# Convolution taps and gate scalings between VectorE, ScalarE and GpSimd, and an earlier second token half, in a hybrid encoder block

## The chip, the cores and the metric

The kernel runs on one core of a Trainium2 chip. The metric is the device time of one execution in microseconds (us); for a kernel with several executions it is their median. The core's engines are TensorE (PE, matrix products and transposes), VectorE (DVE), ScalarE (ACT), GpSimd (POOL) and SyncE (SP, which issues the transfers). Each engine runs its own instructions in program order and waits on semaphores for the others.

## What is computed

One layer of an encoder block, on 1024 tokens of width 1024, all in float32. The part around the change:

```python
h = rms_norm(x, norm1_g)
z = h @ w_in                                   # 1024 x 2560
a, gate, q, k, v = jnp.split(z, splits, axis=-1)   # 512 columns each
u = a * sigmoid(gate)
y = depthwise_conv(u, dw_kernel) + dw_bias     # 31 taps over the tokens, padding 15
conv_out = silu(layer_norm(y, ln_g, ln_b))
q, k = rms_norm per head of 64
attn_out = neighbourhood_attention(q, k, v, rpb)   # 8 heads, 16 rows of 64 tokens
x = x + concat(conv_out, attn_out) @ w_out
h = rms_norm(x, norm2_g)
x = x + (silu(h @ w_gate) * (h @ w_up)) @ w_down
```

## The kernel before

The order of every engine is the order of the code; nothing is rescheduled. All products use split operands: a float32 matrix is held as a high half (a cast) and a low half (the rest), and `mac` (L111 to L114) adds three products: high by high (L112), high by low (L113), low by high (L114). A weight chunk of 128x1024 is loaded raw into one of three buffers; `split` (L104, L108) casts it on ACT and subtracts on POOL, and `take` then issues the load of the chunk three later. The chunks are taken in this order: wk0 to wk3 (the weights of k), then ag10, ag00, ag11, ag01, ag12, ag02, ag13, ag03 (ag1c are gate columns, ag0c value columns of channel chunk c), w00 to w03 (of q), w20 to w23 (of v), then those of w_out. The letters h and l behind a name are its high and low halves, r the raw buffer.

The tokens are worked on in two halves of 512. `h_split` (L258, L259) makes the two halves of the normalised, transposed input for one token half: hT high on ACT, hT low on DVE. The root mean squares of x (tiles of 128 tokens) are not applied to it; they are kept in `r1`, one column for each tile, and applied to the products. `stats1` computes them: for odd tiles with bn_stats on DVE (L264 to L266), for even ones with a Square on ACT (L271), then a Sqrt on ACT (L277) and a reciprocal on DVE (L278). For the gated unit, whose products are channels by tokens, `r_rows` turns four columns of `r1` into a row vector `rb` with four transposes on PE (L287) into a PSUM buffer (tag tp, of two) and a copy on DVE (L288). The same two buffers hold the transposes of q and k (`zt`, L388), which ACT empties (kT at L395, qT at L393).

PE's order in this part: k products of tiles 0 to 3 (first token half); the gated unit of chunk 0, half 0 then half 1, each a gate product (part 0) and a value product (part 1); k tiles 4 to 7; the gated unit of chunks 1 to 3; eight q products (weights w00 to w03); eight v products (w20 to w23); then attention. A product is 24 matmuls into a PSUM bank of 512 columns. Jobs in the list `woven` are taken out between the steps of a product, one after each three matmuls: this is where the transposes of q, k (`head_T`) and the row vector come.

`step(post)` runs behind each product. It does the post-work of the product before, and then calls `side()` once. The post-work of a k or q product (`head_post`) is the squares and a Sqrt on ACT (L366 or L370, L373), three convolution taps on DVE, then zn on DVE (L378 to L381), and it sets the transposes of zn seven places ahead in `woven`. That of a gate product is `gate`: sg = gate x rb on DVE (L440), Sigmoid on ACT (L441), sg x rb on DVE (L442), and taps. That of a value product is `val`: u = value x sg on DVE (L448), and taps.

The convolution of a channel chunk reads u, 128 channels by 1024 tokens. `pump(n)` issues n of DVE's steps: the centre tap into the accumulator cv in PSUM (L312), then one multiply-add for each tap (L317), and at the end u = cv + pa (L322). `side()` issues one tap of the list SIDE: the product on ACT (L342; for the first tap straight into pa, L339) and the addition to pa on POOL (L343). A chunk begins when u of both token halves is there.

Of the kernel before, what the change touches and what calls it, by code (L numbers as in the profile page):

```python
# [8 lines left out]
AF = mybir.ActivationFunctionType  # L9
OP = mybir.AluOpType  # L10
PSUM = bass.MemoryType.PSUM

P = 128
D = 1024
S = 1024
KB = D // P
# [7 lines left out]
NEG = -1e30  # L24
GW = 64
AR = 12
SIDE = (16, 17, 18, 19, 20, 21)
WIN = ((0, 24, 8), (8, 32, 0), (24, 32, 0), (40, 24, 0))


# [37 lines left out]
def build(ctx, tc, a):  # L68
    nc = tc.nc
    pe, act, dve, pool = nc.tensor, nc.scalar, nc.vector, nc.gpsimd  # L70
    sb = ctx.enter_context(tc.tile_pool(name="sb", bufs=1))
# [4 lines left out]
    def T(tag, shape, bufs, name, dt=F32):  # L76
        return sb.tile(shape, dt, tag=tag, bufs=bufs, name=name)

    def G(name, dt=F32):
        return T("G", [P, 1024], 22, name, dt)  # L80
# [7 lines left out]
    def ST(name, dt=F32):  # L88
        return T("st", [P, 512], 5, name, dt)

    def SM(name, n=8):
        return T("sm", [P, 8], 16, name)[:, :n]

    def mm(name):
        return ps.tile([P, 512], F32, tag="mm", bufs=4, name=name)

    def tp(name):
        return ps.tile([P, 512], F32, tag="tp", bufs=2, name=name)

    def cv(name):  # L100
        return ps.tile([P, 1024], F32, tag="cv", bufs=1, name=name)

    def split(hi, lo, src, sub=(pool,)):
        act.copy(hi, src)  # L104
        n = src.shape[-1] // len(sub)
        for i, eng in enumerate(sub):
            sl = slice(i * n, (i + 1) * n)
            eng.tensor_tensor(*[w[..., sl] for w in (lo, src, hi.bitcast(F32))], OP.subtract)  # L108

    def mac(acc, l, r, start, stop):  # L110
        (lh, ll), (rh, rl) = l, r  # L111
        pe.matmul(acc, lh, rh, start=start, stop=False, skip_group_check=True)  # L112
        pe.matmul(acc, lh, rl, start=False, stop=False, skip_group_check=True)  # L113
        pe.matmul(acc, ll, rh, start=False, stop=stop, skip_group_check=True)  # L114


    woven = []

    def weave():
        if woven:  # L120
            woven.pop(0)()
# [12 lines left out]
    def issue():  # L134
        if pos[0] < len(chunks):
            src, name, _, _ = chunks[pos[0]]
            raws[pos[0]] = R(name + "r")
            d = raws[pos[0]]
            if len(src.shape) == 3:
                d = d.rearrange("p (k m) -> p k m", k=src.shape[1])  # L140
            nc.sync.dma_start(d, src)
            pos[0] += 1

    def take(n=1, ahead=True):
        for _ in range(n):
            i = pos[1]
            while pos[0] <= i:
                issue()
            _, _, dst, sub = chunks[i]
            hi, lo = dst()  # L150
            split(hi, lo, raws.pop(i), sub)
            pos[1] += 1
            if ahead and pos[0] < i + 4:
                issue()
# [53 lines left out]
    FIRST, SECOND, ALL = slice(0, 256), slice(256, 512), slice(0, 512)  # L208
# [21 lines left out]
    eps = T("eps", [P, 1], 1, "eps")  # L230
# [22 lines left out]
    r1 = T("r1", [P, 8], 1, "r1")  # L253

    def h_split(h, k, sl):
        src = xr[h, k // 2][:, k % 2, sl]
        hi, lo = [w[:, k, sl] for w in hT[h]]
        act.activation(hi, src, AF.Copy, scale=g1[:, k:k + 1])  # L258
        dve.scalar_tensor_tensor(lo, src, g1[:, k:k + 1], hi.bitcast(F32), OP.mult, OP.subtract)  # L259

    def bn_sum(t):
        st, mv, ss = T("bn", [P, 2, 6], 2, f"sb{t}"), SM(f"sv{t}", 2), SM(f"s1{t}", 1)
        for i in range(2):
            dve.bn_stats(st[:, i], x_t[t][:, i * 512:(i + 1) * 512])  # L264
        dve.bn_aggr(mv, st)
        dve.scalar_tensor_tensor(ss, mv[:, 0:1], mv[:, 0:1], mv[:, 1:2], OP.mult, OP.add)  # L266
        return ss, 1.0
# [6 lines left out]
    def stats1(t):  # L274
        ss, scale = (bn_sum if t % 2 else sq_sum)(t)
        sd = SM(f"sd1{t}", 1)
        act.activation(sd, ss, AF.Sqrt, bias=eps, scale=scale)  # L277
        dve.reciprocal(r1[:, t:t + 1], sd)  # L278
# [3 lines left out]
    def r_rows(h):  # L282
        if not rb:
            rb.append(G("rb"))
        pt = tp(f"rb{h}")
        for i in range(4):
            pe.transpose(pt[:, i * P:(i + 1) * P], r1[:, 4 * h + i:4 * h + i + 1].to_broadcast([P, P]), ident)  # L287
        dve.tensor_copy(rb[0][:, h * 512:(h + 1) * 512], pt)  # L288
# [13 lines left out]
    def span(t):  # L302
        lo, hi = max(0, 15 - t), min(S, S + 15 - t)
        return slice(lo, hi), slice(lo + t - 15, hi + t - 15)

    def conv_taps():
        for c in range(4):
            while len(u) <= c or not u[c][1]:
                yield False
            uc = u[c][0]  # L310
            acc = cv(f"cv{c}")
            dve.tensor_scalar(acc, uc, dwk[:, c, 15:16], dwb[:, c:c + 1], op0=OP.mult, op1=OP.add)  # L312
            yield True
            for t in range(CW):
                if t != 15 and t not in SIDE:
                    o, i = span(t)
                    dve.scalar_tensor_tensor(acc[:, o], uc[:, i], dwk[:, c, t:t + 1], acc[:, o], OP.mult, OP.add)  # L317
                    yield True
            for _ in range(10):
                if len(aside) <= c or not aside[c][1]:  # L320
                    side()
            dve.tensor_tensor(uc, acc, aside[c][0], OP.add)  # L322
            yield True


    aside = []

    def side_taps():
        for c in range(4):
# [4 lines left out]
            aside.append([pa, False])  # L334
            for n, t in enumerate(SIDE):
                o, i = span(t)
# [3 lines left out]
                else:  # L340
                    pr = G(f"pr{c}{t}")
                    act.activation(pr[:, o], uc[:, i], AF.Copy, scale=dwk[:, c, t:t + 1])  # L342
                    pool.tensor_tensor(pa[:, o], pa[:, o], pr[:, o], OP.add)  # L343
                aside[c][1] = n == len(SIDE) - 1
                yield
# [3 lines left out]
    def side():  # L349
        next(sides, None)  # L350

    conv = conv_taps()

    def pump(n):
        for _ in range(n):
            if not next(conv, False):
                return
# [49 lines left out]
    def step(post=None, n_taps=4):  # L407
        todo = pend[:]
        pend.clear()
        if post is not None:  # L410
            pend.append(post)
        behind()
        for f in todo:
            f(n_taps)
        if not todo:
            pump(n_taps)
        side()

    def head_post(n, t, z):
        def f(n_taps):  # L420
            sd = head_sq(n, t, z)
            pump(3)
            zn = head_scale(n, t, z, sd)
            woven.extend([lambda: None] * 6)
            woven.append(lambda: head_T(n, t, zn))
        return f

    def glu_step(c, h, part, accs, extra=None):
        acc = accs[part] = mm(f"gl{c}{h}{part}")
        w = [q.rearrange("p (k m) -> p k m", m=P) for q in wag[1 - part, c][0]]  # L430
        for k in range(KB):
            mac(acc, [q[:, k, :] for q in w], [q[:, k, :] for q in hT[h]], k == 0, k == KB - 1)
            weave()
        if extra:
            extra(0)

        def gate(n_taps):
            sg = accs["sg"] = ST(f"sg{c}{h}")
            row = rb[0][:, h * 512:(h + 1) * 512]
            dve.tensor_tensor(sg, acc, row, OP.mult)  # L440
            act.activation(sg, sg, AF.Sigmoid)  # L441
            dve.tensor_tensor(sg, sg, row, OP.mult)  # L442
            pump(n_taps - 1)

        def val(n_taps):
            if h == 0:
                u.append([G(f"u{c}"), False])
            dve.tensor_tensor(u[c][0][:, h * 512:(h + 1) * 512], acc, accs["sg"], OP.mult)  # L448
            u[c][1] = h == 1
            pump(n_taps)  # L450
        step((gate, val)[part])


# [38 lines left out]
    def behind(n=6):  # L492
        for _ in range(n):
            if aside_dma:
                aside_dma.pop(0)()
# [7 lines left out]
    for kp in range(4):  # L503
# [13 lines left out]
        for j in range(2):  # L517
            for t in range(2):
                k = 2 * kp + j
# [10 lines left out]
    take(1, False)  # L530
    for q in range(4):
        load_xt(1, q, ALL)
    woven.extend([lambda: None] * 4)
    woven.append(lambda: r_rows(0))
    project(1, 3, head_post)
    for t in range(4, 8):
        load_x(t)
    take(1)
    accs = {}
    for part in range(2):  # L540
        glu_step(0, 0, part, accs)
    for k in range(KB):
        h_split(1, k, ALL)
    for t in range(4, 8):
        stats1(t)
    woven.extend([lambda: None] * 4)
    woven.append(lambda: r_rows(1))
    accs = {}
    for part in range(2):
        glu_step(0, 1, part, accs)  # L550
    for t in range(4, 8):
        project(1, t, head_post)
        if t in (4, 6):
# [3 lines left out]
    for c in range(1, 4):  # L557
        for h in range(2):
            accs = {}
# [129 lines left out]
    s1 = score_mm(1)  # L689
# [80 lines left out]
    for i in range(2, 32 + 2):  # L770
# [8 lines left out]
        if i < 32:  # L779
            ss = score_mm(i)  # L780
# [455 lines left out]
```

## Time and profile before

| | us |
|---|---|
| median of three runs | 1087.36 |
| lowest and highest | 1086.7, 1088.07 |
| profiled execution | 1088.63 |
| its span in the trace | 1086.9 |

| engine | busy us | share of the span |
|---|---|---|
| PE | 1058.5 | 97% |
| DVE | 702.1 | 65% |
| ACT | 453.6 | 42% |
| POOL | 382.1 | 35% |

Times in the trace run from the span's start. The stage around the change lies between 30 and 250 us; the gated unit of chunks 1 to 3 between 84.88 and 151.8, the first q product starts at 151.8. Rows of a timeline give the start, the duration, the engine, the line of the kernel, the operation, and in brackets how long the engine was idle before it and what ended that. Rows that say x4 or x7 hold so many instructions.

### The profile page before, as it was taken

To read this page: it belongs to the slowest core of one execution; us is meant where nothing else is said; L and a number is where in the kernel's file an instruction comes from. 1 tells how busy PE (TensorE), PEld (TensorE's weight loads), DVE (VectorE), ACT (ScalarE), POOL (GpSimd) and SP (SyncE) were. 2 spreads that over 40 slices of the span, in tenths; PEclk is the share of its full clock that TensorE was granted. 3 is DMA by queue.
4 is the path that set the end of the run, shared out by engine and by line. 5 is a ranking of instruction groups with operands and counts; after the bars stand their busy time and mean duration, and the time that the engine had idled before them with its cause. 6 is when DMAs were issued, how large, how long until landed. Compare 5 with 4: busy or idle time off the path is not lost.

```text
span 1086.9 us, 14051 instructions
## 1 busy us (share of the span) xinstructions
PE 1058.5 (97%) x5068; PEld 850.6 (78%) x5068; DVE 702.1 (65%) x1054; ACT 453.6 (42%) x993; POOL 382.1 (35%) x299
## 2 busy tenths in 40 slices
PE   7999998999999999999999999999999999999997
PEld 6778886876667788788888888888888888888886
DVE  6577998795675335765645546464564567857883
ACT  6556345825775524542232322323223245433431
POOL 0126374412452201645445444454445300002220
PEclk9999998999999999999999999999999999999999
DMA  9316772144422442123222322322332498624541
GB/s 343 143 45 221 214 197 79 64 160 135 138 86 80 135 136 97 39 74 121 97 95 100 127 97 80 133 97 88 107 110 94 145 326 303 203 80 131 187 151 43
DMA packets 68245, 144.06 MB, mean 133 GB/s; under 512 B 12496, under 2 KB 21200, under 8 KB 67536
## 3 DMA queue, kind: packets, MB, share of 16 engines
q1 hardware_dynamic: 66336, 139.95, 38.5%
q10 hardware_dynamic: 1840, 3.22, 0.9%
q8 instruction: 40, 0.66, 0.3%
q14 instruction: 29, 0.24, 0.1%
HBM read 103.99 MB, written 44.76 MB: 137 GB/s over the span
## 4 chain that ended last, share of the span: by engine, by line
PE 83%; DVE 9%; ACT 4%; issue 2%; DMA 1%; POOL 1%; SPq 0%; ACTq 0%; DVEq 0%; POOLq 0%
PE B L112 6%; PE B L114 6%; PE B L113 6%; DVE cv L317 5%; PE D L112 4%; PE D L114 4%; PE D L113 4%; PE A L112 4%; PE A L114 4%; PE A L113 3%; PE z L112 3%; PE z L113 3%; PE z L114 3%; PE p L637 2%; PE B2d L112 1%
## 5 line engine op out<-in xcount | busy, mean ns | idle before, releaser
L317 DVE SCALAR_TENSOR_TENSOR cv<-u,par,cv 128x1009 f32<-128x1009 f32 (+11 forms) x96 | 122.7, 1278 | 2.7
L104 ACT CAST op<-sr 128x512 fp32r<-128x512 f32 x77 | 47.6, 619 | 51.5 <-PE B2d L114 20.9
L343 POOL TENSOR_TENSOR pa<-pa,pr 128x1022 f32<-128x1022 f32 (+4 forms) x20 | 47.9, 2397 | 59.3 <-ACT pr L342 55.3
L1023 DVE TENSOR_TENSOR g<-B,g 128x512 f32<-128x512 f32 x22 | 15.2, 691 | 80.3 <-PE B L114 80.3
L108 DVE TENSOR_TENSOR op<-sr,op 128x512 fp32r<-128x512 f32 x77 | 56.0, 728 | 16.3 <-ACT op L104 16.3
L1191 POOL TENSOR_TENSOR ou<-ou,resm 128x512 f32<-128x512 f32 x8 | 12.1, 1511 | 143.8 <-DMA resm<-xd 140.6
L1032 ACT ACTIVATE D<-D 128x512 f32<-128x512 f32 x22 | 12.8, 582 | 114.5 <-DVE D L1031 114.5
L1018 DVE TENSOR_TENSOR u<-B,g 128x512 f32<-128x512 f32 x22 | 15.2, 690 | 64.5 <-PE B L114 64.5
L104 ACT CAST op<-wd 128x512 fp32r<-128x512 f32 x66 | 40.9, 619 | 31.7 <-DVE wd L1110 18.5
L108 DVE TENSOR_TENSOR op<-wd,op 128x512 fp32r<-128x512 f32 x66 | 52.5, 796 | 2.2 <-ACT op L104 0.4
L628 POOL TENSOR_SCALAR e<-e,rs 128x288 f32<-128x288 f32 (+1 forms) x64 | 34.3, 548 | 55.3 <-DVE rs L626 25.3
L872 DVE TENSOR_TENSOR ts<-gu,ts 128x512 f32<-128x512 f32 x44 | 53.1, 1208 | 0.8
L1021 ACT ACTIVATE A<-A 128x512 f32<-128x512 f32 x20 | 11.6, 582 | 77.4 <-PE A L114 77.4
L621 ACT ACTIVATE e<-e,mx 128x288 f32<-128x288 f32 (+1 forms) x64 | 36.3, 568 | 8.2 <-DVE mx L619 8.2
L637 PEld LDWEIGHTS p<-ident,e 128*96 128x96 f32 (+1 forms) x192 | 20.0, 133 | 18.6 <-issue 10.3
L872 DVE TENSOR_TENSOR ts<-gu 128x512 f32<-128x512 f32 x22 | 34.1, 1551 | 0.0
L619 DVE CUSTOM_DVE_ANT_0 e<-s,tab 128x288 f32<-128x288 f32 (+1 forms) x64 | 29.8, 503 | 5.9 <-PE s L606 5.4
L637 PE MATMUL p<-ident,e 128*96 128x128 f32 (+1 forms) x192 | 27.5, 279 | 3.9 <-DVE pT L642 2.5
L370 ACT ACTIVATE sq<-z,r 128x64 f32<-128x64 f32 x96 | 28.6, 335 | 2.8 <-PE z L114 2.8
L653 PE MATMUL o<-pT,vw 96*64 96x128 f32 (+1 forms) x384 | 28.0, 281 | 0.0
L606 PE MATMUL s<-kT,qT 64*128 64x288 f32 (+1 forms) x128 | 26.7, 495 | 0.0
L112 PE MATMUL B2d<-op 128*128 128x512 f32 x66 | 25.8, 391 | 0.0
(1033 smaller groups left out, 3470.0 us busy)
## 6 DMA issues: line engine op xcount, KB each, us to landing
gu<-in_gu SPq DMA_DIRECT2D x44, 512.0 KB
sr<-sd SPq DMA_DIRECT2D x77, 256.0 KB
sd<-sd SPq DMA_DIRECT2D x22, 512.0 KB
wd<-in_wd SPq DMA_DIRECT2D x44, 256.0 KB
sd<-g SPq DMA_DIRECT2D x33, 256.0 KB
x<-in_x SPq DMA_DIRECT2D x16, 512.0 KB
xd<-x SPq DMA_DIRECT2D x8, 512.0 KB
resm<-xd SPq DMA_DIRECT2D x16, 256.0 KB
```

The costliest lines, as they stand in the source:

```text
L104: act.copy(hi, src)
L108: eng.tensor_tensor(*[w[..., sl] for w in (lo, src, hi.bitcast(F32))], OP.subtract)
L112: pe.matmul(acc, lh, rh, start=start, stop=False, skip_group_check=True)
L113: pe.matmul(acc, lh, rl, start=False, stop=False, skip_group_check=True)
L114: pe.matmul(acc, ll, rh, start=False, stop=stop, skip_group_check=True)
L317: dve.scalar_tensor_tensor(acc[:, o], uc[:, i], dwk[:, c, t:t + 1], acc[:, o], OP.mult, OP.add)
L343: pool.tensor_tensor(pa[:, o], pa[:, o], pr[:, o], OP.add)
L619: dve.tensor_tensor_reduce(out=e[:, hh], in0=ss[hh], in1=tab[rh, cb][2 * hp + hh], scale=-1.0, scalar=3.0e38, op0=OP.add, op1=OP.min, accu ...
L621: act.activation(e[:, hh], e[:, hh], AF.Exp, bias=mx, scale=-1.0, accum_out=rs[:, hh:hh + 1])
L628: pool.tensor_scalar(es[i][:, hh], es[i][:, hh], rs[:, hh:hh + 1], 1.0, op0=OP.mult, op1=OP.mult)
L637: pe.transpose(pt[:m, g * P:(g + 1) * P], es[i][:, hh, g * m:(g + 1) * m], ident)
L872: dve.tensor_tensor(o, l, r, OP.subtract)
```

## The change

SIDE grows from six taps to nine, so DVE has 21 multiply-adds in each chunk instead of 24. `step` calls `side()` a second time once the side taps of the second chunk have begun. The second scaling in `gate` is on POOL. `gate` and `val` both pump three taps (before: three and four). In the first part, the row vector of half 0 is made straight ahead of the first gate product rather than woven into a k product; the split of the second token half stands around the first gate product, ahead of the post-work that holds the first Sigmoid; the statistics of tiles 4 to 7 are all by bn_stats on DVE, with a single Sqrt and a single reciprocal of four columns; the row vector of half 1 is made right behind the gate product of half 1.

```diff
-SIDE = (16, 17, 18, 19, 20, 21)
+SIDE = (16, 17, 18, 19, 20, 21, 22, 23, 24)
...
-    def bn_sum(t):
-        st, mv, ss = T("bn", [P, 2, 6], 2, f"sb{t}"), SM(f"sv{t}", 2), SM(f"s1{t}", 1)
+    def bn_sum(t, ss=None):
+        st, mv = T("bn", [P, 2, 6], 2, f"sb{t}"), SM(f"sv{t}", 2)
+        ss = SM(f"s1{t}", 1) if ss is None else ss
...
-            for _ in range(10):
+            for _ in range(2 * len(SIDE)):
                 if len(aside) <= c or not aside[c][1]:
                     side()
...
         if not todo:
             pump(n_taps)
         side()
+        if len(aside) > 1:
+            side()
...
             act.activation(sg, sg, AF.Sigmoid)
-            dve.tensor_tensor(sg, sg, row, OP.mult)
-            pump(n_taps - 1)
+            pool.tensor_tensor(sg, sg, row, OP.mult)
+            pump(3)
...
             u[c][1] = h == 1
-            pump(n_taps)
+            pump(3)
...
-    woven.extend([lambda: None] * 4)
-    woven.append(lambda: r_rows(0))
     project(1, 3, head_post)
     for t in range(4, 8):
         load_x(t)
     take(1)
+    r_rows(0)
+    for k in range(4):
+        h_split(1, k, ALL)
     accs = {}
-    for part in range(2):
-        glu_step(0, 0, part, accs)
-    for k in range(KB):
+    glu_step(0, 0, 0, accs)
+    for k in range(4, KB):
         h_split(1, k, ALL)
+    ss = SM("s14", 4)
     for t in range(4, 8):
-        stats1(t)
-    woven.extend([lambda: None] * 4)
-    woven.append(lambda: r_rows(1))
+        bn_sum(t, ss[:, t - 4:t - 3])
+    act.activation(ss, ss, AF.Sqrt, bias=eps)
+    dve.reciprocal(r1[:, 4:], ss)
+    glu_step(0, 0, 1, accs)
     accs = {}
-    for part in range(2):
-        glu_step(0, 1, part, accs)
+    glu_step(0, 1, 0, accs, lambda _: r_rows(1))
+    glu_step(0, 1, 1, accs)
```

## The prediction

> **What bounds the kernel now.** I read the busy shares first, then what TensorE (PE) waits for, then the timeline around those waits, then the busy time by stages.
>
> ```profile
> PE 1058.5 (97%) x5068; PEld 850.6 (78%) x5068; DVE 702.1 (65%) x1054; ACT 453.6 (42%) x993; POOL 382.1 (35%) x299
> ```
>
> PE is busy for 97% of the span, so only two things can move the end: time in which PE waits, and time in which it runs at a lower clock. The waits, by PE line and releaser (us, times, longest):
>
> ```profile
> PE z L112 <- ACT wk0h L104: 6.1, 1, 6.1
> PE zt L388 <- DVE zn L381: 4.8, 1, 4.8
> PE rb L287 <- ACT kT L395: 1.9, 1, 1.9
> PE gl L112 <- ACT hT L258: 0.7, 1, 0.7
> PE gl L113 <- DVE hT L259: 0.3, 1, 0.3
> ```
>
> The first is the start-up, which the change does not touch. The other four, 7.7 us, are what it is about; around the second and third the clock falls too:
>
> ```profile
> 43.71 0.40 PE L114 MATMUL gl<-hT,ag00l 128*128 128x512 f32 x1
> ...
> 55.82 0.40 PE L114 MATMUL gl<-hT,ag00l 128*128 128x512 f32 x1
> 58.16 0.65 PE L287 MATMUL rb<-ident,r 128*128 128x128 f32 x4 [1.94 <-ACT kT L395]
> 58.56 0.48 PE L112 MATMUL gl<-hT,ag00h 128*128 128x512 f32 x1
> 60.72 0.63 PE L112 MATMUL z<-wk0h,hT 128*128 128x512 f32 x1
> 62.42 0.50 PE L113 MATMUL z<-wk0l,hT 128*128 128x512 f32 x1
> 62.76 0.39 PE L114 MATMUL z<-wk0h,hT 128*128 128x512 f32 x1
> 67.19 0.39 PE L112 MATMUL z<-wk0h,hT 128*128 128x512 f32 x1
> ...
> 172.87 1.11 PE L388 MATMUL zt<-ident,zn 128*128 128x128 f32 x4 [4.81 <-DVE zn L381]
> 178.81 0.39 PE L112 MATMUL z<-w01h,hT 128*128 128x512 f32 x1
> 182.75 0.39 PE L112 MATMUL z<-w00h,hT 128*128 128x512 f32 x1
> ```
>
> The columns are start, duration, engine, line, operation, and the wait before it. Matmuls start 0.233 us apart at full clock (the 24 of one product reach from 60.72 to 67.19; the last nineteen steps, from 62.76 on, take 4.43) and 0.425 apart after a wait (four steps from 60.72 to 62.42). So the wait before 58.16 also cost some 1.5 us of slow matmuls, and the one before 172.87 some 2.5 (some thirteen slow steps up to 178.81). The wait at 172.87 is VectorE's (DVE) fault:
>
> ```profile
> 151.80:175.06 23.26, 18.45 (x78) 14.62 (x77) 22.00 (x22) 9.69 (x28) 11.98 (x7) 0.93 0.63 181
> 162.49 9.15 DVE L317 SCALAR_TENSOR_TENSOR cv<-u,par,cv 128x1010 f32<-128x1010 f32 x7
> ```
>
> In this stretch (columns: its length, then busy PE, PEld, DVE, ACT, POOL, then clock) DVE is busy 22.00 of 23.26 us, and seven convolution taps stand ahead of zn. GpSimd (POOL) is busy 11.98, so there is room to move work; but POOL also makes the low halves of the weights, for which PE has to wait.
>
> **The change, part by part.** *The early reorder.* In it DVE makes four low halves of hT ahead of zn of k tile 3, the other four straight after it, then four sets of bn statistics; then come one Sqrt, one reciprocal and rb.
>
> ```profile
> 34.48 2.39 POOL L108 TENSOR_TENSOR ag00l<-ag00r,ag00h 128x1024 fp32r<-128x1024 f32 x1 [2.14 <-ACT ag00h L104]
> ...
> 39.74 0.69 DVE L381 TENSOR_TENSOR zn<-z,r 128x512 f32<-128x512 f32 x1
> 44.83 5.39 DVE L259 SCALAR_TENSOR_TENSOR hT<-xt,par,hT 128x512 fp32r<-128x512 f32 x8
> 51.44 0.29 ACT L277 ACTIVATE sd<-s,eps 128x1 f32<-128x1 f32 x1
> 51.85 1.27 DVE L264 BATCH_NORM_STATS2 sb<-x 128x6 f32<-128x512 f32 x2
> 53.40 0.22 DVE L266 SCALAR_TENSOR_TENSOR s<-sv 128x1 f32<-128x1 f32 x1
> 57.43 1.25 ACT L395 ACTIVATE kT<-zt,par 128x512 f32<-128x512 f32 x2
> ```
>
> If nothing hinders DVE, zn ends at 40.4 as before and four halves of 5.39/8 = 0.67 at 43.1. Both hT waits go, because the products of half 1 come later than that. One set of statistics takes 1.77 (51.85 to 53.62); four end at 50.2. ScalarE (ACT) does the Sqrt (0.3, as sd at 51.44) and then kT, which has waited behind it and holds the PSUM bank that rb needs: 0.62, so rb can start at 51.2. PE would be there at 49.95 (the last matmul of half 0 starts at 43.71, so half 1 begins at 43.94; 24 matmuls of 0.233 and four transposes of 0.4 in all follow). A wait of 1.25 stays where 1.94 was. Then rb 0.4 (58.16 to 58.56) and 24 x 0.233 = 5.6: the first k product of half 1 starts at 57.2, not 60.72, and with the clock held the next one at 62.8, against 67.19, a lead of 4.4.
>
> But something does hinder DVE, by one row:
>
> ```profile
> 99.03 1.27 DVE L442 TENSOR_TENSOR sg<-sg,rb 128x512 f32<-128x512 f32 x1 [3.33 <-ACT sg L441]
> 97.34 2.42 POOL L108 TENSOR_TENSOR ag12l<-ag12r,ag12h 128x1024 fp32r<-128x1024 f32 x1
> L442 DVE TENSOR_TENSOR sg<-sg,rb x8: 691/693/1274, 44.2 to 157.5; 128x512 f32<-128x512 f32 x8
> ```
>
> Eight scalings of two SBUF tiles (last row: shortest, median, longest in ns) take 0.69 but for the one that began while POOL ran a split; that one ended 0.54 after the split's end, as if it had been held until then. The low halves of hT too read two SBUF tiles, and in the new order the first four are due at 35, inside POOL's split of ag00 (34.48 to 36.87). Held until 36.87 they end at 39.55, the reduction for tile 3 behind them comes 1.44 later than its 38.11 in before, and all that follows with it: rb at 52.65, a wait of 2.7, the first k product of half 1 at 58.65. After a wait that is longer than 1.94 the clock falls as it did: the lead is 2.1 with the fall, 3.5 without. I take 2.1, and 1.5 to 4.4 as its bounds.
>
> The Trainium skill has this as a rule (SBUF — State Buffer, "Who interferes with whom"): a DVE instruction with two SBUF inputs and a GpSimd instruction that reads SBUF share an interface, and whichever comes second waits for the whole of the other. The row at 99.03 agrees. It speaks against the early half of the change, and for taking sg x rb away from DVE; the taps have one input in PSUM, so by the rule they are not hindered.
>
> *Three more side taps a chunk, and the second scaling on POOL.* DVE loses twelve taps of 1.31 (9.15/7) and eight scalings of 0.69 in all. POOL gains twelve adds and eight scalings; ACT gains twelve products. The durations:
>
> ```profile
> 123.94 4.91 POOL L343 TENSOR_TENSOR pa<-pa,pr 128x1022 f32<-128x1022 f32 x2 [3.06 <-ACT pr L342]
> 140.37 2.42 POOL L108 TENSOR_TENSOR w00l<-w00r,w00h 128x1024 fp32r<-128x1024 f32 x1
> 142.74 2.43 POOL L108 TENSOR_TENSOR w01l<-w01r,w01h 128x1024 fp32r<-128x1024 f32 x1
> L923 POOL TENSOR_TENSOR xn<-xn,sn 128x512 f32<-128x512 f32 x4 | 5.2, 1292 | 0.0
> L1191 POOL TENSOR_TENSOR om<-om,resm 128x512 f32<-128x512 f32 x4 | 6.9, 1749 | 13.8 <-DMA resm<-xd 13.8
> 98.90 1.13 ACT L342 ACTIVATE pr<-u,par 128x1018 f32<-128x1018 f32 x1
> 114.42 1.23 DVE L322 TENSOR_TENSOR u<-cv,pa 128x1024 f32<-128x1024 f32 x1
> ```
>
> A tap is 2.42, a split 2.37 (140.37 to 142.74). The scaling is not in this trace; a 128x512 product or sum on POOL runs from 1.29 to 1.75. I take 1.25, half of a 2.42 tap and nearest to the 1.29 of L923. From the end of ag12l's split (99.7 before, 97.6 with the lead of 2.1) to the end of w03l's, POOL's program order holds sixteen taps, seven splits and five scalings: 38.7 + 16.6 + 6.3 = 61.6. One pause lies inside: chunk 1's first add needs chunk 0's last one, behind which come DVE's final add (1.23), the second half of u (0.7), the base product and the first product on ACT (1.13 each), 4.2 in all. So w03l is ready at 97.6 + 65.8 = 163.4. PE needs the three late ones at:
>
> ```profile
> 135.77 0.39 PE L114 MATMUL gl<-hT,ag03l 128*128 128x512 f32 x1
> 154.83 0.39 PE L113 MATMUL z<-w02l,hT 128*128 128x512 f32 x1
> 156.23 0.39 PE L113 MATMUL z<-w03l,hT 128*128 128x512 f32 x1
> ```
>
> Each less 2.1. By the same sum ag03l comes at 134.6 against 133.7 (0.9 late), w02l at 156.4 against 152.7 + 0.9 (2.8 late), w03l at 163.4 against 154.1 + 3.7 (5.6 late). In all 9.3 us of new waits on POOL stand in front of the q tiles, whatever the lead is. From there: two more steps of w03 (1.2), q tile 1 (5.6), tiles 2 and 3 (6.0 each with their transposes): the fifth q product starts at 182.2 if the clock holds. After a wait of 5.6 it falls as it did after 4.8; 1.5 to 2.5 were seen, I take 2.0: 184.2, against 182.75. zn of q tile 0 is no longer late: POOL's last scaling ends at 164.7, u's second half on DVE (0.7, as zn) at 165.4, then the six taps that stand before zn in program order, 7.9, and 1.1 for r and zn: 174.4. PE asks for it at 164.6 + 5.6 + 5.6 = 175.8. This is a cover of 1.4 us, and if it goes, each further us is paid.
>
> Behind POOL's scaling stands u on DVE (L448), and the taps behind that.
>
> ```profile
>   ACT sg L441: 9.6, 8
> ```
>
> That is how long DVE idled before the eight scalings (us, times); it does so no more, and has 12 x 1.31 + 8 x 0.69 = 21.2 us less to do. By the sum above it waits for POOL four times in turn, some 4, 4, 7 and 7. That leaves it 9 us better, so the last final add comes no later than before. On ACT the q steps hold twelve products instead of ten, 2.3 us at 1.13: 0 to 2.3 on the path. I take 0, because ACT is busy 9.69 of 23.26 in the stretch at 151.80. The raw loads on SP's queue wait for the split that frees their buffer, three chunks back: w03r's comes free with w00l, seven POOL instructions or 15 us ahead of its own split. From the fifth q product on the order is the same.
>
> The sum: +1.45 us on the profiled execution's span of 1086.9. That execution took 1088.63, 1.73 more than its span and 1.27 more than the median; I set the difference against the median: 1087.36 + 1.45 = 1088.8.
>
> **The rivals.** *Slower beyond doubt: POOL's queue is longer than this.* If a scaling takes 1.75 as L1191's does, five cost 2.5 more; ACT's q steps cost up to 2.3. The mechanism is one: POOL's chain to w03l has no slack, so each us that it gains reaches PE. It decides when the chain exceeds 67 us. With the scalings alone: 1088.8 + 2.5 = 1091.3. For it: rows of 128x512 on POOL reach 1749. Against: taps hold 2.42 under a full DVE.
>
> *Faster: the splits come in time.* If the waits on POOL were not there, 9.3 + 2.0 less would be paid, 1077.5; half of it gives 1083. For it: the wait of 4.8 with its slow clock is gone in either case, and POOL's spans are rough, so a tap may cost less than its 2.42 in a full queue. Against: POOL's order is fixed, and 61.6 us of work stand in it.
>
> *The early part is worth all of its 4.4,* nothing holds DVE and the clock stays: 1088.8 - 2.3 = 1086.5. For it: only one row shows DVE held. This is inside what I call no change.
>
> **How the numbers follow.** The likeliest, POOL's queue takes back what the removed waits give: 0.40, with its own range 1086.5 to 1091; the early part worth all of its 4.4: 0.10. The longer queue 0.26; splits in time 0.24. The measurement tells a change from none at about 0.2%, 2.2 us, so at 1085.2 and 1089.6. All of the third rival and 0.26 of the likeliest case lie between, 0.14 of it above: the same 0.36, slower 0.26 + 0.14 = 0.40, faster 0.24. The range goes from somewhat beyond half-paid splits, 1081.5, to the longer queue with 1.7 of ACT's 2.3, 1093.
>
> **What would show it.** PE's waits: none on hT; rb about 2.7 (1.3 if DVE isn't held); zt on zn gone; new ones on ag03l, w02l and w03l of about 1, 3 and 6, released by POOL's split. The first four low halves of hT take 0.67 each but the first, which is long or starts late. POOL without a pause from 97 to 163 but one of 4. The scaling near 1.25. If PE's waits on w02l and w03l are missing, or if the sixteen taps are longer than 2.5 each, the sum is wrong.

## The result, and the profile after

The changed kernel took 1092.46 us (median of six runs, 1091.63 to 1093.77) beside 1088.05 us for the kernel before in the same comparison: a ratio of 1.0039, 95% interval 1.0026 to 1.0052, some 4.2 us slower. Its profiled execution, the slowest of the six, took 1093.77 us with a span of 1091.9, 5.0 more than the span of before.

The page's first part, the busy shares:

```profile
PE 1058.7 (97%) x5068; PEld 850.7 (78%) x5068; DVE 685.3 (63%) x1039; ACT 459.9 (42%) x996; POOL 419.3 (38%) x319
```

DVE is rid of 17 us, as meant, and POOL has 37 more. PE's work is the same 1058 us, so the 5 us are waits and slow matmuls. PE's waits in the changed kernel (us, times, longest):

```profile
PE z L112 <- ACT wk0h L104: 6.8, 1, 6.8
PE z L113 <- POOL w03l L108: 5.4, 1, 5.4
PE zt L389 <- DVE zn L382: 2.6, 2, 1.3
...
PE z L113 <- POOL w02l L108: 2.4, 1, 2.4
...
PE rb L288 <- ACT kT L396: 1.9, 1, 1.9
...
PE gl L114 <- POOL ag03l L108: 0.9, 1, 0.9
```

The one wait of 4.8 on zn and the two on hT are gone. In their place stand three on POOL's splits, 8.7 in all, and two of 1.3 on zn. The first line, the start-up, was 0.7 shorter in the profiled execution before; over the profiles of this study it ran from 6.1 to 8.4, so it belongs to the execution and not to the kernel.

POOL's timeline from ag12l's split to w03l's:

```profile
96.31 2.44 POOL L108 TENSOR_TENSOR ag12l<-ag12r,ag12h 128x1024 fp32r<-128x1024 f32 x1
98.69 1.32 POOL L445 TENSOR_TENSOR sg<-sg,rb 128x512 f32<-128x512 f32 x1
...
117.52 2.41 POOL L344 TENSOR_TENSOR pa<-pa,pr 128x1022 f32<-128x1022 f32 x1 [4.18 <-ACT pr L343]
...
157.44 4.80 POOL L344 TENSOR_TENSOR pa<-pa,pr 128x1020 f32<-128x1020 f32 x2
162.20 2.34 POOL L108 TENSOR_TENSOR w03l<-w03r,w03h 128x1024 fp32r<-128x1024 f32 x1
```

From the end of ag12l (98.75) to that of w03l (164.54) it is 65.8 us, with one pause of 4.18 in it; all else is back to back. The two adds at 157.44 stand between the splits of w02 and w03 while PE waits for w03. On PE:

```profile
53.02 0.65 PE L288 MATMUL rb<-ident,r 128*128 128x128 f32 x4 [1.86 <-ACT kT L396]
...
157.54 0.50 PE L113 MATMUL z<-w02l,hT 128*128 128x512 f32 x1 [2.42 <-POOL w02l L108]
...
164.59 0.80 PE L113 MATMUL z<-w03l,hT 128*128 128x512 f32 x1 [5.40 <-POOL w03l L108]
...
185.95 0.39 PE L112 MATMUL z<-w00h,hT 128*128 128x512 f32 x1
192.32 0.63 PE L389 MATMUL zt<-ident,zn 128*128 128x128 f32 x4 [1.30 <-DVE zn L382]
```

The fifth q product starts at 185.95 instead of 182.75, and the two waits on zn come behind it, at 192.32 and 205.90. What makes these late is on DVE:

```profile
36.25 4.21 DVE L259 SCALAR_TENSOR_TENSOR hT<-xt,par,hT 128x512 fp32r<-128x512 f32 x4
42.54 2.73 DVE L259 SCALAR_TENSOR_TENSOR hT<-xt,par,hT 128x512 fp32r<-128x512 f32 x4
...
189.43 0.20 DVE L379 RECIPROCAL r<-d 128x8 f32<-128x8 f32 x1 [1.34 <-ACT d L374]
189.66 1.71 DVE L380 TENSOR_SCALAR r<-r,r 128x8 f32<-128x8 f32 x1
191.48 0.69 DVE L382 TENSOR_TENSOR zn<-z,r 128x512 f32<-128x512 f32 x1
203.24 1.72 DVE L380 TENSOR_SCALAR r<-r,r 128x8 f32<-128x8 f32 x1
```

A multiplication on 128x8, which takes 0.23 elsewhere, took 1.71 and 1.72 just ahead of zn. The reciprocal just before it, on as many elements, took its usual 0.20. On POOL at those times:

```profile
188.95 2.40 POOL L108 TENSOR_TENSOR w21l<-w21r,w21h 128x1024 fp32r<-128x1024 f32 x1
...
202.52 2.40 POOL L108 TENSOR_TENSOR w22l<-w22r,w22h 128x1024 fp32r<-128x1024 f32 x1
```

The two splits end at 191.35 and 204.92, the small multiplications at 191.37 and 204.96: DVE was held to the end of POOL's instruction. A third one, for q tile 0, took 1.11 from 174.38 and ended with an add of a side tap at 175.5; PE did not wait for that zn. The four low halves of hT at 36.25 are 1.5 longer than the four at 42.54 for the same reason: the split of ag00 ran from 35.52 to 37.92.

### The profile page after: what moved, and what is told of

Its sections match the earlier page's. It is cut to its first block, busy times and chain, and to the rows that moved or that the text cites. A ratio compares the mean times of both kernels' runs of the same rounds, so it can differ in the third digit from the quotient of the medians.

```text
span 1091.9 us, 14072 instructions
## 1 busy us (share of the span) xinstructions
PE 1058.7 (97%) x5068; PEld 850.7 (78%) x5068; DVE 685.3 (63%) x1039; ACT 459.9 (42%) x996; POOL 419.3 (38%) x319
## 4 chain that ended last, share of the span: by engine, by line
PE 83%; ACT 5%; DVE 4%; POOL 4%; issue 3%; DMA 0%; SPq 0%; POOLq 0%; ACTq 0%; DVEq 0%
PE B L112 6%; PE B L114 6%; PE B L113 6%; PE D L112 4%; PE D L114 4%; PE D L113 4%; PE A L112 4%; PE A L114 4%; PE z L112 3%; PE A L113 3%; PE z L113 3%; PE z L114 3%; POOL pa L344 2%; PE p L642 2%; PE B2d L112 1%
## 5 line engine op out<-in xcount | busy, mean ns | idle before, releaser
L318 DVE SCALAR_TENSOR_TENSOR cv<-u,par,cv 128x1009 f32<-128x1009 f32 (+14 forms) x84 | 107.3, 1277 | 2.2
L344 POOL TENSOR_TENSOR pa<-pa,pr 128x1022 f32<-128x1022 f32 (+7 forms) x32 | 76.5, 2392 | 28.2 <-ACT pr L343 27.0
L108 DVE TENSOR_TENSOR op<-wd,op 128x512 fp32r<-128x512 f32 x66 | 49.5, 750 | 1.6 <-ACT op L104 0.2
L343 ACT ACTIVATE pr<-u,par 128x1022 f32<-128x1022 f32 (+7 forms) x32 | 34.8, 1132 | 0.0
```

## Experiments: the parts by themselves

The theory at this point: POOL's queue from ag12l to w03l, 65.8 us long, sets when PE gets through the first q product, and POOL holds DVE up in rows like those at 36.25 and 189.66. The first four kernels undo, keep or change one part. Each ratio is to the kernel before on the same chip. Where two profiles are compared below, "net" means that the difference at 31 us, which the start-up made, is taken out.

*The early reorder alone*: six side taps, scaling on DVE and one side tap a step, as before.

```diff
 SIDE = (16, 17, 18, 19, 20, 21)
...
+    r_rows(0)
+    for k in range(4):
+        h_split(1, k, ALL)
     accs = {}
+    glu_step(0, 0, 0, accs)
+    for k in range(4, KB):
+        h_split(1, k, ALL)
...
```

> Before with the early reorder alone (six side taps, scaling on DVE, one side tap a step). Theory: the reorder is worth a lead of about 2 us at the k tiles of half 1 (rb waits about 1.9 and the clock falls behind it); nothing on POOL is late, DVE still holds zn of q tile 0 and its taps start about 1 to 2 us sooner, so 1 to 2 us less than before, ratio about 0.998 to 0.999. Rival: DVE's zn sets the end of this stage whatever PE does ahead of it, then the lead is lost in a longer wait on zn: ratio 1.000, and the wait on zn 2 us longer than 4.8.

Measured: 1085.23, ratio 0.9975 (0.9965 to 0.9984), so 2.9 us less than before, somewhat more than expected. PE's waits:

```profile
PE zt L389 <- DVE zn L382: 4.8, 1, 4.8
...
PE rb L288 <- ACT kT L396: 1.6, 1, 1.6
```

The wait on zn is as long as before and comes 2.7 sooner (170.14 instead of 172.87): DVE's queue moved along with the lead. The rival, that zn takes the lead back, is out. Net, the lead is 3.7; the clock held behind rb's wait of 1.6, and the prediction has 3.5 for that case.

*The early reorder undone* in the changed kernel (nine side taps, scaling on POOL).

> The changed kernel with the early reorder undone. Theory: waits on hT (0.7, 0.3) and rb (1.9) come back, the lead of 2 us is gone, and the POOL chain from ag12l to w03l starts 2 us later and stays 65.8 long: 1.5 to 2.5 us over the changed kernel, ratio to before about 1.006. Rival: the chain's length does not decide and the lead is eaten by the waits on w02l and w03l: same time as the changed kernel, with these waits about 2 us shorter.

Measured: 1093.65, ratio 1.0052 (1.0038 to 1.0065), 1.2 to 1.4 us over the changed kernel. That is less than the theory's 1.5 to 2.5, and the two intervals overlap. The waits on w02l and w03l stayed at 2.4 and 5.3, so the rival's sign, shorter waits, is not there. But the profiles do not show the theory's lead either: rb waited 1.37 here and the clock held behind it, while it fell in the changed kernel, and at 84.9 us PE is ahead of the kernel before by 2.0 net here and by 2.1 there. What the early reorder is worth beside the other two parts stays open.

*The scaling back on DVE* in the changed kernel.

```diff
-            pool.tensor_tensor(sg, sg, row, OP.mult)
+            dve.tensor_tensor(sg, sg, row, OP.mult)
```

> The changed kernel with the second scaling back on DVE. Theory (POOL's queue decides): the chain loses five scalings of 1.29, w03l comes 6.4 us sooner, the waits on ag03l, w02l, w03l of 0.9, 2.4, 5.4 shrink to 0 to 2.5 together: 5 to 6 us less than the changed kernel, ratio to before about 0.999. Rival (DVE and POOL hold each other): the scaling on DVE then meets POOL at work almost always, takes 1.5 to 3 instead of 0.69, u and the taps come later, zn of q tile 0 is late again by 2 to 5 us: ratio 1.002 to 1.004.

Measured: 1091.47, ratio 1.0032 (1.0019 to 1.0045). The time is the rival's, but its path came true only in part. The scaling on DVE in this kernel (shortest, median, longest in ns):

```profile
L445 DVE TENSOR_TENSOR sg<-sg,rb x8: 692/1006/2899, 54.8 to 154.6; 128x512 f32<-128x512 f32 x8
```

In the kernel before the same row was 691/693/1274. So DVE was held, as the rival says, though in half of the rows only; zn of q tile 0, which it expected late by 2 to 5, was not waited for. PE waited for ag03l (2.0), for w03l (4.8), and twice for zn behind the small multiplication (1.3 each). POOL is held in turn: its four adds behind sg of chunk 2 took longer than in the changed kernel, 10.32 instead of 9.86, and so did a split:

```profile
107.96 4.86 POOL L344 TENSOR_TENSOR pa<-pa,pr 128x1016 f32<-128x1016 f32 x2 [3.52 <-ACT pr L343]
...
121.77 10.32 POOL L344 TENSOR_TENSOR pa<-pa,pr 128x1021 f32<-128x1021 f32 x4
132.05 2.82 POOL L108 TENSOR_TENSOR ag03l<-ag03r,ag03h 128x1024 fp32r<-128x1024 f32 x1
```

With a second pause of 3.52, because ACT's products stand behind a Sigmoid that DVE feeds later (its sg ended 9.4 after the end of ag12l, and 6.4 in the changed kernel), POOL's chain from ag12l to w03l is 65.3 us long (96.74 to 161.99): five scalings less, and the same length. That is why the theory's gain did not come.

*The small multiplication folded* into the operation behind it, in the changed kernel.

```diff
-        dve.tensor_scalar(r, r, r1[:, t:t + 1], None, op0=OP.mult)
...
-        dve.tensor_tensor(zn, z, r[:, :, None].to_broadcast([P, NH, HD]), OP.mult)
+        dve.scalar_tensor_tensor(zn, z, r1[:, t:t + 1], r[:, :, None].to_broadcast([P, NH, HD]), OP.mult, OP.mult)
```

> The changed kernel with the multiplication of r by r1 (128x8, SBUF to SBUF) folded into the operation that makes zn. Theory: that small instruction took 1.1 to 1.7 instead of 0.23 where a POOL tap was running, and this made zn late for PE twice by 1.3 in the q tiles; without it the two waits go: 2 to 2.6 us less than the changed kernel, ratio to before about 1.0015. Rival: the two products a step on ACT make zn late; then the waits stay at 1.3 each and the time is the same.

Measured: 1089.14, ratio 1.0007 (0.9998 to 1.0016), 3.4 us less than the changed kernel. No wait on zn is left in PE's list, though ACT still makes two products a step: the rival, that ACT makes zn late, is out. The operation that makes zn now holds the multiplication by r1 and reads z from PSUM. It ran beside the same two splits and was not held; the first of them (the second: 0.75 from 198.08, inside w22l's 197.32 to 199.73):

```profile
185.22 2.40 POOL L108 TENSOR_TENSOR w21l<-w21r,w21h 128x1024 fp32r<-128x1024 f32 x1
186.00 0.75 DVE L381 SCALAR_TENSOR_TENSOR zn<-z,r,r 128x512 f32<-128x512 f32 x1
```

The two multiplications that PE had waited for were held by splits; the expectation's taps held only the one of 1.11. The gain is more than the 2.6 of the two waits. In this profile the clock held behind rb, whose wait was 1.1, and PE was 1.8 further ahead, net, at 84.9 us than in the changed kernel; how much of that is the fold's and how much chance of the execution was not separated.

## Experiments: order and load on POOL

*The splits ahead of the taps.* In the changed kernel, chunks 1 to 3: `take` runs behind the matmuls and ahead of `step`.

```diff
-                glu_step(c, h, part, accs)
-                if c < 3 and part == 0 or c == 3 and (h, part) != (1, 1):
-                    take(2 if c == 3 and h == part == 0 else 1)
+                n = (c == 3 and (h, part) != (1, 1) or c < 3 and part == 0) + (c == 3 and h == part == 0)
+                glu_step(c, h, part, accs, lambda _, n=n: take(n))
```

> The changed kernel with the splits of the gated unit's chunks 1 to 3 issued ahead of the step's taps and scaling, and nothing else. Theory: ag13l fills POOL's pause of 4.2, w03l comes about 7 us sooner, the waits on splits shrink from 8.7 to 1 to 2 and the clock no longer falls behind them; the two waits on zn in the q tiles (1.3 each) stay: 7 to 9 us less than the changed kernel, 1084 to 1086, ratio 0.997 to 0.998. Rival (total load): the wait moves to zn of q tile 0; within 3 us of the changed kernel.

Measured: 1088.37, ratio 1.0001 (0.9992 to 1.001), 4.1 us less than the changed kernel, between the 7 to 9 of the theory and the 3 of its rival. Each had one sign right: the waits on splits went, and a wait on zn of q tile 0 came.

```profile
PE zt L389 <- DVE zn L382: 6.5, 4, 4.6
```

The splits come in time but for 1.8 on w03l. Now the scaling stands behind the taps instead, and the last one ends at 161.54; u, six taps and zn follow it, and the wait of 4.6 on zn of q tile 0 is back.

*The same with fewer taps in the crowded chunk*: splits ahead, one side tap a step in chunk 3, and the fold.

```diff
-        if len(aside) > 1:
+        if len(aside) > 1 and not slow:
             side()
```

Here `slow` holds an entry while chunk 3 is worked on.

> The changed kernel with every split of the gated unit's chunks 1 to 3 issued ahead of the step's taps and scaling, one side tap a step in chunk 3, and r x r1 folded into zn. Theory (the splits are late because they stand behind taps in POOL's queue): the waits on ag03l, w02l, w03l (8.7) and the slow clock behind them (about 2) go, and the two waits on zn (2.6): about 1079 to 1081, ratio 0.992 to 0.994. Rival (POOL's total load decides, the order does not): the scaling and so u come later instead, zn of q tile 0 is waited for by 4 or more, and the time is 1085 to 1089, ratio 0.997 to 1.001.

Measured: 1080.22, ratio 0.9924 (0.9913 to 0.9936). The time is the theory's. No split of q's weights is waited for, and zn of q tile 0 costs 1.2; one split of v's weights, w23l, is now late by 0.9. It has the same nine taps, and POOL is as busy: from 95 to 160 us 60.35 of 65 here and 60.11 in the changed kernel. So with the same load on POOL the waits went: what stood in front of what in POOL's queue made them. From ag12l's split to w03l's the queue is 59.1 us long here (90.84 to 149.94) instead of 65.8, with thirteen adds in it instead of sixteen. The kernel has three edits; what each is worth in it was not measured.

*Six side taps*, one a step, with the pumps as before; the early reorder and the scaling on POOL stay.

```diff
-SIDE = (16, 17, 18, 19, 20, 21, 22, 23, 24)
+SIDE = (16, 17, 18, 19, 20, 21)
...
         side()
-        if len(aside) > 1:
-            side()
...
-            pump(3)
+            pump(n_taps - 1)
...
-            pump(3)
+            pump(n_taps)
```

> The changed kernel with six side taps, one side tap a step and the pumps as before; the early reorder and the scaling on POOL stay. Theory: six adds, two splits and two scalings a chunk are about 20 of POOL's 22 us, so the splits are in time up to w01l and w03l at most 2 late; DVE is rid of a scaling and of the wait for the Sigmoid ahead of it, 1.4 a half, and zn of q tile 0 comes some 5 us sooner: 4 to 6 us less than the early reorder alone, 1079 to 1082, ratio 0.992 to 0.995. Rival: the scaling waits behind a tap on POOL and holds u, so DVE gains nothing and zn is waited for as before: 1085, ratio 0.9975.

Measured: 1077.54, ratio 0.9903 (0.989 to 0.9916), 7.7 us less than the early reorder alone, from which it differs only by the engine of the scaling, and more than the 4 to 6 expected. In the two profiles PE is level, net, up to q tile 0 and 7.7 apart at the fifth q product. Of these, 4.8 are the wait on zn and 2.4 the slow matmuls behind it, which only the early reorder alone has. Besides the start-up, PE waits once up to the attention:

```profile
PE rb L288 <- ACT kT L396: 1.9, 1, 1.9
```

Nothing waits for zn and nothing for a split. POOL's window (length, then busy PE, PEld, DVE, ACT, POOL) shows why there is room:

```profile
95.00:160.00 65.00, 65.00 (x285) 53.15 (x284) 62.14 (x57) 27.77 (x45) 48.74 (x26) 1.00 0.76 232
```

POOL is busy 48.74 of 65, DVE 62.14; in the kernel before DVE was busy 57.15 in the same window, with holes in which it waited for a Sigmoid. The move of the scaling filled these holes; the three further side taps were not needed for it.

*Seven side taps*, otherwise the last kernel.

> The six-tap kernel with seven side taps, one side tap a step. Theory (POOL's load decides): w03l's split ends at 146 and is wanted near 153; three more adds ahead of it (7.2) use up that margin, so w03l is 0 to 1.5 late and the time is 0 to 3 us over the six-tap kernel, ratio 0.990 to 0.993. Rival (the bursts of two side taps a step do the harm, not the load): no wait on a split, the same as six taps or better.

Measured: 1077.57, ratio 0.9895 (0.9881 to 0.991): as with six. w03l's split ended at 147.6 and nothing waited for it. POOL's margin is larger than I had put it, and the run does not tell load from bursts.

*The taps alone*: nine, two a step and three pumps, with the early part and the scaling as before.

> The changed kernel with the early reorder undone and the scaling on DVE: nine side taps, two a step, three pumps alone. Theory (POOL is the bound with nine taps, whoever scales, and the scaling on DVE is held by POOL): about as the kernel with the scaling on DVE plus what the early reorder gave, 1092 to 1095, ratio 1.004 to 1.007. Rival (the parts add up): the early reorder is worth 2.9 and the scaling on POOL 7.7 of the time between six taps and the early reorder alone, so the taps alone are some 14.7 slower than before: 1103.

Measured: 1094.23, ratio 1.0049 (1.0036 to 1.0063), as the theory said, far from 1103. The parts do not add up. In ratios to before:

| early reorder | scaling on POOL | nine taps, two a step, three pumps | ratio |
|---|---|---|---|
| - | - | - | 1 |
| yes | - | - | 0.9975 |
| yes | yes | - | 0.9903 |
| - | - | yes | 1.0049 |
| yes | - | yes | 1.0032 |
| - | yes | yes | 1.0052 |
| yes | yes | yes | 1.0039 |

The early reorder is worth 0.25% by itself; beside nine taps the difference is 0.13 and 0.17%, and the intervals overlap. The scaling on POOL is worth 0.7% with six taps and nothing with nine. The taps cost 0.5 to 0.6% where DVE scales, and 1.4% where POOL does. The scaling on POOL without the early reorder and with six taps wasn't run.

## Experiments: the early part

*The hT splits ahead of ag00's split*, in the early reorder alone.

```diff
-    take(1)
     r_rows(0)
     for k in range(4):
         h_split(1, k, ALL)
+    take(1)
```

> The early reorder alone with the first four splits of hT issued ahead of the split of ag00, so that no POOL split runs beside their low halves. Theory (DVE is held by POOL): the four low halves take 2.7 instead of 4.2, the statistics and rb come 1 to 1.5 sooner, rb's wait falls from 1.6 to 0.5 or less: 1 to 3 us less than the early reorder alone if zn of q tile 0 moves with it, ratio 0.995 to 0.997. Rival: ag00's split comes too late for its first product (a wait of 1 or more there), or the low halves take 4.2 still, and the time is that of the early reorder alone, 0.9975.

Measured: 1084.46, ratio 0.9967 (0.9955 to 0.9979), an interval that overlaps that of the early reorder alone. What the rival names is what happened. The four low halves took 4.87, not 2.7. POOL's split was not late enough: it ran from 37.55 to 40.14, and the last half was held by it. PE also waited 0.8 for ag00l. The order did not remove the hold, so the run tells nothing of what its absence would be worth.

*Two of the four statistics on ACT*, in the kernel with six side taps.

```diff
-        bn_sum(t, ss[:, t - 4:t - 3])
+        if t % 2:
+            bn_sum(t, ss[:, t - 4:t - 3])
+        else:
+            act.activation(cv(f"j{t}"), x_t[t], AF.Square, scale=D ** -0.5, accum_out=ss[:, t - 4:t - 3])
```

> The kernel with six side taps (early reorder and scaling on POOL kept), with the statistics of tiles 4 and 6 as a Square on ACT instead of bn_stats on DVE. Theory (rb waits because four sets of statistics stand in a row on DVE while ACT idles 8 us): two sets less on DVE, 3.5 us, the Sqrt, kT and rb come 2 us or more sooner, the wait on rb of 1.9 and the slow clock behind it (1.5) go: 2.5 to 3.5 us less than with six taps, 1074 to 1075, ratio 0.987 to 0.988. Rival: kT waits for something else, rb stays 1 late or more, the same 1077.5.

Measured: 1075.7, ratio 0.9884 (0.9868 to 0.99). In that profile rb starts at 50.30 with no wait. Its interval overlaps that of the six-tap kernel, so the gain in time, 2 us by the ratios where 2.5 to 3.5 were expected, is likely and not certain; that the wait went is plain.

*The same with the fold.*

> As the last, and r x r1 folded into zn. Theory: with six taps POOL no longer runs beside that small instruction when PE waits for zn (no wait on zn in the six-tap kernel), so the fold is worth 0 to 0.6: 1073.5 to 1075. Rival: it still hides a hold, 1 us or more less.

Measured: 1076.13, ratio 0.9885 (0.9869 to 0.9902), the same as without it, as expected: in the kernel without it none of the sixteen small multiplications was held. These two, seven taps and six taps have intervals that overlap, 1.0 to 1.2% below the kernel before and 1.4 to 1.5% below the changed one.

## Why the prediction came out as it did

The forecast was 1088.8 with a range of 1081.5 to 1093, slower the likeliest of the three. The kernel came out slower, at 1092.46 inside the range, 3.7 above the forecast. By the ratio the change cost 4.2 where 1.45 was worked out, so some 2.7 are missing in the sum.

- *The early part.* The waits on hT went. The hold of DVE by ag00's split was there: the first four low halves took 1.5 more, and the reduction and all behind it moved with them. PE and POOL's split were both 1.0 later from the start in that execution. rb was ready at 53.02 where the sum has 52.65, so the work up to rb took 0.7 less than reckoned, and the wait was 1.9 and not 2.7. The clock fell behind it. At the second k product of half 1 PE was 1.0 ahead of the kernel before, 2.1 net, against a lead of 2.1.
- *POOL's chain.* 65.8 forecast, 65.8 measured; the pause 4.2 and 4.18; the scaling 1.25 and 1.28 to 1.32. The waits on ag03l, w02l and w03l were forecast as 0.9, 2.8 and 5.6 and came as 0.9, 2.4 and 5.4. This term carried the forecast, and it was right because the program order of POOL was counted instruction by instruction. The slow matmuls behind w03l cost 2.5 where the sum put 2.0 (from 164.59 twelve steps took 5.29, and 2.80 at full pitch). The fifth q product came 3.2 later than before, 2.1 net, against 1.45.
- *DVE's waits for POOL.* Four of 4, 4, 7 and 7 were forecast; the long ones measured were 7.0, 4.5, 4.4 and 6.5, the first of them for the last add of chunk 0 and the others for a scaling. zn of q tile 0 was in time, as forecast.
- *The term that was missing:* "I take 0, because ACT is busy 9.69 of 23.26 in the stretch at 151.80". The bound of 0 to 2.3 was put on ACT's products. In its place came two waits of 1.3 on zn in the q tiles, and the fold shows that they were due to DVE's 128x8 multiplication, held by the splits of w21 and w22, and not to ACT. The hold itself had been seen in the row at 99.03 and was applied to hT, but not to the other DVE instructions that would now meet a busy POOL. With the wait and the step behind it each cost PE 1.5: the lag grew from 3.2 to 6.2 us between the fifth q product and 210 us.
- *The rivals, and the luck in it.* The longer queue did not come, and the splits were not in time. The forecast's case was the right one, and a term was missing in it. Its sum alone, 1088.8, lies in what it calls no change (1085.2 to 1089.6); slower was the likeliest because of the longer queue, and the upper part of the range was there for that queue and for ACT's products. The measured time fell there for another reason, so that it lies in the range is partly luck.

*What hid a part of it.* At the end of the span the lag is 5.0 and not 6.2. The rest came back in the attention, in rows of the kernel before:

```profile
344.07 2.39 POOL L108 TENSOR_TENSOR wo<-wo02r,wo 128x1024 fp32r<-128x1024 f32 x1 [3.15 <-ACT wo L104]
344.19 2.28 DVE L742 SCALAR_TENSOR_TENSOR bb<-bm,br 128x1 f32<-128x1 f32 x1
347.42 0.66 PE L715 MATMUL y<-ident,u 128*128 128x128 f32 x4 [1.47 <-ACT xh L743]
```

An operation on 128x1 (0.16 at 347.38) was held to the end of a split, xh came late, and PE waited 1.5 for it. In the profile of the changed kernel that wait is 0.3. So the kernel before had such a hold on PE's path too, and neither the forecast nor the change was about it. Net, the span is 4.0 longer where the sum has 1.45: 0.7 up to the fifth q product and 3.0 at the two waits on zn, less these 1.2.

The Trainium skill (SBUF — State Buffer, "Who interferes with whom") bears on the small multiplication too: beside DVE instructions with two SBUF inputs it lists copies, casts and tensor_scalar, in modes in which they take the pair of ports that GpSimd uses, and whichever starts second waits for the whole of the other. The rows of 1.71 and 1.72 agree with it, though the trace does not name the mode. The taps (one input in PSUM) ran at 1.26 to 1.29 in every kernel here, beside POOL too, which agrees as well.

## What to carry to other kernels

Where an engine makes what the bounding engine needs, list everything that stands ahead of it in that engine's own queue: here the changed kernel, in which adds stand before splits, was 0.4% slower than before, and the nine-tap kernel with the splits first, a thinner crowded chunk and the fold was 0.8% faster. Before giving GpSimd more work, go through all VectorE instructions that will then run beside it, the smallest too, and see which of them can be held. A move that frees an engine of a wait (the scaling) can be worth more than one that frees it of work (the taps), so run the parts apart before keeping them together.

## What was not expected of the hardware

The hold can turn an instruction of 0.23 us into one of 1.7, and one of 0.16 into 2.28. It depends on the operation: beside the same two splits the reciprocals on 128x8 took their 0.20 and the multiplications on 128x8 were held. It goes both ways: a POOL split took 2.82 instead of 2.4 beside a scaling on DVE that had begun 0.16 earlier.

The clock did not follow the length of a wait. In the changed kernel matmuls kept full pitch behind the wait of 2.42 at 157.54 and started 0.43 apart behind that of 1.86 at 53.02. The kernels with six and with seven side taps have the same program up to that place, and the same wait there:

```profile
53.80 0.65 PE L288 MATMUL rb<-ident,r 128*128 128x128 f32 x4 [1.86 <-ACT kT L396]
...
54.74 0.40 PE L114 MATMUL gl<-hT,ag00l 128*128 128x512 f32 x1
54.98 0.40 PE L112 MATMUL gl<-hT,ag00h 128*128 128x512 f32 x1
```

```profile
52.69 0.65 PE L288 MATMUL rb<-ident,r 128*128 128x128 f32 x4 [1.87 <-ACT kT L396]
53.09 0.62 PE L112 MATMUL gl<-hT,ag00h 128*128 128x512 f32 x1
53.51 0.63 PE L113 MATMUL gl<-hT,ag00h 128*128 128x512 f32 x1
```

With six taps (the first rows) matmuls soon start 0.23 apart again; with seven they are 0.43 apart for eight steps, which costs 1.6. The Trainium skill (TensorE: Matmul & The Clock Gate, "Part 1: The HAM clock gate") says that activity is watched in a window that runs freely. That would explain why the same wait lowers the clock in one execution and not in another; these rows agree with it, and no run here shows the window itself. An estimate that adds slow matmuls to each wait is good to about 1.5 us, and so is a comparison of two single profiles.
